# Two-layer diffusion trunk on one core: the first FFN's convolution moves to PSUM, its down-projection gets row buffers of its own, and the last FFN is ordered tile by tile

## The chip, the cores and the metric

The kernel runs on one core of a Trainium2 chip. The core has five engines that each work through their own instructions in order: TensorE (PE; its weight loads are PEld), VectorE (DVE), ScalarE (ACT), GpSimd (POOL) and SyncE (SP), which here only issues DMAs. SBUF is the core's on-chip memory of 128 partitions; PSUM is eight banks of 128 x 512 f32 into which TensorE writes its sums and which DVE and ACT read and write. The metric is device microseconds of one execution; lower is better.

## The reference

A trunk of two layers runs on 768 tokens of width 1024: 512 latent ones and 256 of context. Layer 0 mixes tokens by multi-head latent attention, layer 1 by neighbourhood attention; each mixer is followed by a gated feed-forward block (FFN) with a convolution, and each block ends with a residual sum and a layer norm:

```
def conv_ffn(h, w_in, conv_w, conv_b, w_out):
    u = h @ w_in
    u = lax.conv_general_dilated(
        u, conv_w[:, None, :].astype(u.dtype), window_strides=(1,),
        padding=[(FFN_CONV // 2, FFN_CONV // 2)],
        dimension_numbers=('NWC', 'WIO', 'NWC'),
        feature_group_count=u.shape[-1]) + conv_b
    a, g = jnp.split(u, 2, axis=-1)
    return (jax.nn.silu(g) * a) @ w_out
```

`w_in` takes 1024 to 2 x 2816 features and `w_out` 2816 back to 1024; the convolution has three taps a channel and runs over latent and context tokens apart (so 511 and 255 neighbours). The first FFN is that of layer 0, on all 768 tokens; the last is that of layer 1, on the latent 512.

## The kernel before

Everything is f32. For TensorE an operand is split in a high part (rounded by a cast on ACT) and a low part (the rest, a subtraction on DVE or POOL), and a product is three matmuls: high x high, low x high, high x low. `load` (L112) brings 1 MB of weights through SP into one of two raw buffers.

The first FFN's up-projection has the hidden width in 22 chunks. A chunk is one Strassen-Winograd step with seven products of twelve matmuls of 128x384 (`product`, L895): the feature side is split in quadrants and their sums S1 to S4 (`sums`, L834 to L837, hi/lo parts L849 and L851), the weight side in B11 to B22 and their sums T1 to T4 on DVE (`weights`, L863 to L866, casts L873 on ACT, low parts L875 on POOL). P1 and P2 add up in the PSUM tile `x`, the other five in the two halves of `yz`. ACT copies P1 from `x` to `s` (L906); DVE adds from PSUM (L903) write the chunk's two halves `ct` of 128x768.

`finish` does the convolution: ACT writes `w1*ct+b` into an SBUF tile `ut` (L927, 128x768), DVE adds the two neighbours in place (L929 and L931, each on 511 and 255 columns, for both halves: eight instructions), ACT applies Silu in place (L934), DVE multiplies the halves to `hm` (L936), and SP stores it as a row of `hid` in DRAM (L937).

The down-projection reads `hid` back: for each half of the tokens and each of eleven pairs of chunks `u`, SP loads `hr` (L971, 393 KB), ACT casts it to `hh` (L984), DVE subtracts to `hl` (L985), and 36 matmuls of 128x512 (L133 to L135, `yps`) follow. These buffers (`fd0`) lie on the left stack of SBUF, opened after the buffers of the up-projection have been closed.

The last FFN (`ffn`, L1047 to L1150) keeps its convolution's input `u` in PSUM, adds into SBUF (L1047), and ends with the sum into `acc` (L1133), the statistics (L676), and the layer norm (L1142, L1150) of four row tiles.

What stands in which order on an engine is set by the framework's scheduler, which simulates a timeline as the program is built; buffers and their number limit what it can place early.

Of the kernel before, what the change touches and what calls it, by code (L numbers as in the profile page):

```python
# [44 lines left out]
def trunk(ctx, tc, x, cx, cc, ada_w, ada_b, vec, ln1_g, ln1_b, ln2_g, ln2_b, w_in, w_out, m_in, m_qb,  # L45
# [44 lines left out]
    sil = const.tile([128, KD, 32], F32, name="sil")  # L90
    nc.vector.memset(sil, 0.0)
    nc.scalar.activation(sil[:, :, 0:2], cct, AF.Silu)
# [39 lines left out]
    def mm3(ps, ah, al, bh, bl, start, stop):  # L132
        nc.tensor.matmul(ps, ah, bh, start=start, stop=False)  # L133
        nc.tensor.matmul(ps, ah, bl, start=False, stop=False)  # L134
        nc.tensor.matmul(ps, al, bh, start=False, stop=stop)  # L135
# [84 lines left out]
    adap, close_ada = pool("adap", side="right")  # L220
    pw, close_pw = pool("pw", side="right")
# [473 lines left out]
    def to_features(z, t, s, slot, dst, wp):  # L695
# [16 lines left out]
        if not slot:  # L712
# [5 lines left out]
            else:  # L718
                sums(t % 3, nc.vector if t == 5 else nc.gpsimd)
# [49 lines left out]
    def mixer_out(layer, slot, o, w_o, nt, wl=None, us=(), done=(), banks=()):  # L769
# [10 lines left out]
        for t in range(nt):  # L780
            s = int(t >= 4)
            tl = slice(t * 128, t * 128 + 128)
            xt = wp.tile([128, D], F32, name="xr", tag="xr", bufs=2)
# [35 lines left out]
    quads, aq = {}, {}  # L819

# [9 lines left out]
    def sums(j, eng):  # L830
        j = slice(j * 128, j * 128 + 128)
        a11, a12, a21, a22 = (quads[q][:, :, j] for q in ((0, 0), (0, 1), (1, 0), (1, 1)))
        s1 = quads["S1"][:, :, j]
        eng.tensor_tensor(s1, a21, a22, op=ALU.add)  # L834
        eng.tensor_tensor(a21, a11, a21, op=ALU.subtract)
        eng.tensor_tensor(a11, s1, a11, op=ALU.subtract)
        eng.tensor_tensor(a12, a12, a11, op=ALU.subtract)  # L837

    def ffn0():
        sq, close_sq = pool("sq", side="left")  # L840
        hl = [acp.tile([128, KD * C], F32R, name="ac" + i, tag="ac" + i, bufs=1) for i in "hl"]
        aq["A22"] = [w[:, :1536].rearrange("p (k n) -> p k n", k=4) for w in hl]
        for n, (nm, q) in enumerate((("S2", (0, 0)), ("S1", "S1"), ("S3", (1, 0)), ("A22", (1, 1)), ("S4", (0, 1)))):
            if nm != "A22":
                aq[nm] = [sq.tile([128, 4, 384], F32R, name=nm + i) for i in "hl"]
            hi, lo = aq[nm]
            for j in range(3):
                sl = slice(j * 128, j * 128 + 128)
                nc.scalar.copy(hi[:, :, sl], quads[q][:, :, sl])  # L849
                e = nc.gpsimd if (n + j) % 2 else nc.vector  # L850
                e.tensor_tensor(lo[:, :, sl], quads[q][:, :, sl], f(hi[:, :, sl]), op=ALU.subtract)  # L851
# [4 lines left out]
        def weights(c, nm):  # L856
            if c not in raws:
                raws[c] = load(w_in[0, c])
            q = {n: raws[c][:, 512 * i:512 * i + 512] for i, n in enumerate(("B11", "B12", "B21", "B22"))}
            if nm[0] == "T" and c not in tts:  # L860
                tt = hp.tile([128, 3, 512], F32, name="tt", tag="tt", bufs=2)
                t3, t2, t4 = (tt[:, i] for i in range(3))
                nc.vector.tensor_tensor(t3, q["B22"], q["B12"], op=ALU.subtract)  # L863
                nc.vector.tensor_tensor(t2, t3, q["B11"], op=ALU.add)
                nc.vector.tensor_tensor(q["B12"], q["B12"], q["B11"], op=ALU.subtract)
                nc.vector.tensor_tensor(t4, q["B21"], t2, op=ALU.subtract)  # L866
                tts[c] = {"T1": q["B12"], "T2": t2, "T3": t3, "T4": t4}
# [6 lines left out]
            e = nc.vector if c < 2 and nm in ("B21", "T1", "T4") else nc.gpsimd  # L874
# [3 lines left out]
        def product(c, p):  # L878
            a, b = PRODUCTS[p]
            wh, wl = weights(c, b)  # L880
            ah, al = aq[a]
# [10 lines left out]
            for k in range(4):  # L892
                ks = slice(k * 128, k * 128 + 128)
                for m, (w, x_) in enumerate(((wh, ah), (wl, ah), (wh, al))):
                    nc.tensor.matmul(ps, w[:, ks], x_[:, k], start=first and k == 0 and m == 0,  # L895
                                     stop=k == 3 and m == 2, skip_group_check=True)

            def tmp(nm):
                d[nm] = hp.tile([128, 384], F32, name=nm, tag=nm, bufs=2)
# [20 lines left out]
        def finish(c):  # L920
            cw = vt[:, CW + c * 6:CW + c * 6 + 6]
            cb = vt[:, CB + c * 2:CB + c * 2 + 2]
            ut = [None, None]
            for i in (1, 0):
                p = prod[c]["c", i]
# [609 lines left out]
```

## Time and profile before

| what | value |
|---|---|
| median of 3 runs | 1858.76 us (1855.51 to 1859.38) |
| profiled execution, its own time | 1858.97 us |
| its span | 1857.0 us |
| busy PE / DVE / POOL / ACT in the span | 91% / 66% / 54% / 48% |
| mixer's output of layer 0 ends, first FFN's products begin | 493.74 us |
| first FFN, last up product | 897.61 us |
| first FFN, first down product | 917.16 us |
| span's last DVE instructions | from 1851.39 us |

A row of a timeline gives the start, the duration, engine, line, operation, and output and inputs by the program's names; x2 is two such instructions in a row; in brackets stands the idle time of the engine before it and the one that released it. A row of a line's group gives the duration of one as least, median and most in ns.

### The profile page before, as it was taken

The page shows a single profiled execution, that of the slowest core. Times are in us where ns is not written, and L with a number is a line of the kernel's source. Part 1 is how long each engine was busy: PE and PEld are TensorE (multiplying, and loading weights), DVE is VectorE, ACT ScalarE, POOL GpSimd, SP SyncE. Part 2 cuts the span into 40 slices and gives each one's busy share as a digit, 9 for nine tenths or more (in the row PEclk, how much of TensorE's full clock was granted, in tenths as well). Part 3 has the DMA queues.
Part 4 walks back from the last instruction along what each step waited for, and adds up shares of the span by engine and source line. Part 5 has one row for each costly group of instructions (what it writes and reads, how often), then busy time and mean ns, then how long its engine had stood idle before and what let it go on. Part 6 is the DMA issues. An engine that isn't in the chain of part 4 may idle for free. (4 is left out here: it accounts for less than half of the span.)

```text
span 1857.0 us, 25938 instructions
## 1 busy us (share of the span) xinstructions
PE 1697.8 (91%) x9512; PEld 1472.1 (79%) x9512; DVE 1220.5 (66%) x2086; ACT 891.1 (48%) x1800; POOL 1010.9 (54%) x913
## 2 busy tenths in 40 slices
PE   6999999989778988998499998899998899999996
PEld 4887787878678988888388778899887788888875
DVE  4477777785688888888615443667664834465776
ACT  3366666672544444434234435676673444333431
POOL 3224334242665656656465946687694745467442
PEclk8999999999989999999799998999998899999998
DMA  8224455234212221222555442111113423223321
GB/s 312 101 103 171 157 196 194 108 115 153 75 46 94 94 91 67 92 94 94 200 171 188 170 145 89 54 55 55 52 55 103 173 88 109 96 79 138 112 80 46
DMA packets 46583, 214.21 MB, mean 115 GB/s; under 512 B 4952, under 2 KB 13032, under 8 KB 28408
## 3 DMA queue, kind: packets, MB, share of 16 engines
q1 hardware_dynamic: 43288, 202.07, 30.8%
q10 hardware_dynamic: 3168, 10.49, 1.6%
q8 instruction: 75, 1.23, 0.3%
q14 instruction: 52, 0.43, 0.1%
HBM read 194.42 MB, written 18.15 MB: 114 GB/s over the span
## 5 line engine op out<-in xcount | busy, mean ns | idle before, releaser
L129 POOL TENSOR_TENSOR wl<-raw,wh 128x512 fp32r<-128x512 f32 x246 | 332.0, 1380 | 195.8 <-ACT wh L125 195.6
L125 ACT CAST wh<-raw 128x512 fp32r<-128x512 f32 x272 | 149.3, 621 | 118.3 <-PE u L134 68.8
L875 POOL TENSOR_TENSOR wl<-raw,wh 128x512 fp32r<-128x512 f32 x84 | 126.9, 1524 | 82.5 <-ACT wh L873 82.5
L493 POOL TENSOR_SCALAR e<-e,st 128x768 f32<-128x768 f32 (+1 forms) x96 | 75.4, 786 | 168.1 <-DVE st L492 143.4
L133 PE MATMUL u<-axh,wh 128*128 128x512 f32 (+1 forms) x384 | 143.8, 375 | 4.4 <-DVE z L800 3.3
L134 PE MATMUL u<-axl,wh 128*128 128x512 f32 (+1 forms) x384 | 143.6, 375 | 0.6 <-POOL axl L732 0.6
L135 PE MATMUL u<-axh,wl 128*128 128x512 f32 (+1 forms) x384 | 143.4, 374 | 0.0
L875 POOL TENSOR_TENSOR wl<-tt,wh 128x512 fp32r<-128x512 f32 x64 | 93.4, 1472 | 58.8 <-ACT wh L873 58.8
L133 PE MATMUL yps<-wh,hh 128*128 128x512 f32 x264 | 106.5, 403 | 19.2 <-ACT hh L984 19.2
L134 PE MATMUL yps<-wl,hh 128*128 128x512 f32 x264 | 105.5, 400 | 0.0
L985 DVE TENSOR_TENSOR hl<-hr,hh 128x128 fp32r<-128x128 f32 (+2 forms) x55 | 38.1, 744 | 101.6 <-ACT hh L984 101.6
L135 PE MATMUL yps<-wh,hl 128*128 128x512 f32 x264 | 104.3, 397 | 0.0
L929 DVE SCALAR_TENSOR_TENSOR ut<-ct,vt,ut 128x511 f32<-128x511 f32 x88 | 87.2, 1031 | 16.1 <-ACT ut L927 16.0
L511 DVE TENSOR_TENSOR pl<-ptr,ph 128x512 fp32r<-128x512 f32 x112 | 76.3, 687 | 21.8 <-ACT ph L507 20.3
L931 DVE SCALAR_TENSOR_TENSOR ut<-ct,vt,ut 128x511 f32<-128x511 f32 x88 | 89.5, 1047 | 0.0
L133 PEld LDWEIGHTS u<-axh,wh 128*128 128x128 f32 x384 | 73.3, 191 | 17.3 <-DVE z L800 3.5
L134 PEld LDWEIGHTS u<-axl,wh 128*128 128x128 f32 x384 | 73.4, 191 | 13.5 <-POOL axl L732 0.9
L487 ACT ACTIVATE e<-sc,st 128x768 f32<-128x768 f32 (+1 forms) x96 | 73.7, 767 | 21.6 <-PE ptr L500 10.2
L135 PEld LDWEIGHTS u<-axh,wl 128*128 128x128 f32 x384 | 73.3, 191 | 12.5
L480 DVE TENSOR_REDUCE st<-sc 128x1 f32<-128x768 f32 (+1 forms) x96 | 73.8, 774 | 14.3 <-PE sc L135 13.4
L507 ACT CAST ph<-ptr 128x512 fp32r<-128x512 f32 x112 | 64.4, 587 | 36.7 <-PE ptr L500 28.2
L1133 DVE TENSOR_TENSOR acc<-ops,acc 128x512 f32<-128x512 f32 x72 | 48.4, 684 | 49.6 <-PE ops L135 49.4
(576 smaller groups left out, 5638.5 us busy)
## 6 DMA issues: line engine op xcount, KB each, us to landing
raw<-w_in SPq DMA_DIRECT2D x44, 1024.0 KB
raw<-ada_w SPq DMA_DIRECT2D x40, 1024.0 KB
raw<-w_out SPq DMA_DIRECT2D x33, 1024.0 KB
raw<-n_qkv SPq DMA_DIRECT2D x12, 1024.0 KB
hid<-hm SPq DMA_DIRECT2D x22, 384.0 KB
hr<-hid SPq DMA_DIRECT2D x22, 384.0 KB
rr<-resid ACTq DMA_DIRECT2D x10, 512.0 KB
raw<-ada SPq DMA_DIRECT2D x4, 1024.0 KB
```

The costliest lines, as they stand in the source:

```text
L125: nc.scalar.copy(hi[:, a:b], raw[:, a:b])
L129: e.tensor_tensor(lo[:, a:b], raw[:, a:b], f(hi[:, a:b]), op=ALU.subtract)
L133: nc.tensor.matmul(ps, ah, bh, start=start, stop=False)
L134: nc.tensor.matmul(ps, ah, bl, start=False, stop=False)
L135: nc.tensor.matmul(ps, al, bh, start=False, stop=stop)
L480: nc.vector.tensor_reduce(st[:, 0:1], ps[:, :n], axis=AX.X, op=ALU.max, negate=True)
L487: done["a"] = nc.scalar.activation(e[:, :n], ps[:, :n], AF.Exp, bias=st[:, 0:1], scale=1.0, accum_out=st[:, 1:2]).ins
L493: done["p"] = nc.gpsimd.tensor_scalar(e[:, :n], e[:, :n], st[:, 2:3], 1.0, op0=ALU.mult, op1=ALU.mult).ins
L511: nc.vector.tensor_tensor(pl, tr, f(ph), op=ALU.subtract)
L875: e.tensor_tensor(lo, src, f(hi), op=ALU.subtract)
L929: nc.vector.scalar_tensor_tensor(u[:, a + 1:b], p[:, a:b - 1], cw[:, 3 * i:3 * i + 1], u[:, a + 1:b], op0=ALU.mult, op1=ALU.add)
L931: nc.vector.scalar_tensor_tensor(u[:, a:b - 1], p[:, a + 1:b], cw[:, 3 * i + 2:3 * i + 3], u[:, a:b - 1], op0=ALU.mult, op1=ALU.add)
```

## The change

- `finish`: the convolution's running value lies in PSUM: `ul` (two banks, 512 latent columns of each half) and `uc` (one bank, 256 context columns of both). ACT's two instructions of 768 columns become four of 512 and 256, Silu reads PSUM and writes `hm` in two pieces, and DVE multiplies `hm` by the other half in PSUM in two pieces. `uc` shares its two banks with `x`.
- `fd`, the down-projection's row buffers, is opened first, below those of the up-projection, with one `hr` in place of two and two `hh`/`hl` in place of three.
- `sums` gives S1, S3, S2, S4 in this order (S2 is now a22 - S3), the last tile's sums stand in `ffn0` between the splits, S1, S2 and S4 are split on DVE, S3 and A22 on POOL, and P5 comes before P6 in the first two chunks.
- `tp`, a pool opened before the mixer's last part, holds `tt` and `s1`, and T4 is written over B21 just before P4; `w_in` is laid out B11, B12, B22, B21.
- In layer 0 `xr` has one buffer in place of two, and `sil` lies in another pool.
- In the last FFN the products of a later row tile are issued after the last one of the tile before.

The diff, cut to its core (the new lines are some 14 to 20 higher: L895 is now L910, L929 and L931 are L946 and L948, L984 is L1001):

```diff
@@ sums @@
-        eng.tensor_tensor(s1, a21, a22, op=ALU.add)
-        eng.tensor_tensor(a21, a11, a21, op=ALU.subtract)
-        eng.tensor_tensor(a11, s1, a11, op=ALU.subtract)
-        eng.tensor_tensor(a12, a12, a11, op=ALU.subtract)
+        for nm, dst, x_, y_, op in (("S1", quads["S1"][:, :, j], a21, a22, ALU.add),
+                                    ("S3", a21, a11, a21, ALU.subtract), ("S2", a11, a22, a21, ALU.subtract),
+                                    ("S4", a12, a12, a11, ALU.subtract)):
+            eng.tensor_tensor(dst, x_, y_, op=op)
+            yield nm
@@ ffn0 @@
+        fd, close_fd = pool("fd0", side="left")
         sq, close_sq = pool("sq", side="left")
...
+        for nm in sums(2, nc.vector):
+            if nm == "S1":
+                split("S1", nc.vector, 3)
+            elif nm == "S2":
+                split("S2", nc.vector, 3)
+                split("S3", nc.gpsimd, 3)
+        split("A22", nc.gpsimd, 3)
+        split("S4", nc.vector, 3)
@@ weights @@
-                tt = hp.tile([128, 3, 512], F32, name="tt", tag="tt", bufs=2)
+                tt = tp.tile([128, 2, 512], F32, name="tt", tag="tt", bufs=2)
...
+            if nm == "T4":
+                nc.vector.tensor_tensor(q["B21"], q["B21"], tts[c]["T2"], op=ALU.subtract)
@@ finish @@
-                ut[i] = u = hp.tile([128, T], F32, name=f"ut{i}", tag=f"ut{i}", bufs=2)
-                nc.scalar.activation(u, p, AF.Identity, bias=cb[:, i:i + 1], scale=cw[:, 3 * i + 1:3 * i + 2])
...
-                if i:
-                    nc.scalar.activation(u, u, AF.Silu)
+            ul = [bank("ul", [128, 512], "tr") for i in range(2)]
+            uc = bank("uc", [128, 512])
+            ut = [[(ct[i][:, :S], ul[i]), (ct[i][:, S:], uc[:, C * i:C * i + C])] for i in range(2)]
             for i in (1, 0):
+                for p, u in ut[i]:
+                    n = u.shape[-1]
+                    nc.scalar.activation(u, p, AF.Identity, bias=cb[:, i:i + 1], scale=cw[:, 3 * i + 1:3 * i + 2])
+                    nc.vector.scalar_tensor_tensor(u[:, 1:], p[:, :n - 1], cw[:, 3 * i:3 * i + 1], u[:, 1:],
+                                                   op0=ALU.mult, op1=ALU.add)
+                    nc.vector.scalar_tensor_tensor(u[:, :n - 1], p[:, 1:], cw[:, 3 * i + 2:3 * i + 3], u[:, :n - 1],
+                                                   op0=ALU.mult, op1=ALU.add)
-            nc.vector.tensor_tensor(hm, ut[0], ut[1], op=ALU.mult)
+            for a, b, k in ((0, S, 0), (S, T, 1)):
+                nc.scalar.activation(hm[:, a:b], ut[1][k][1], AF.Silu)
+                nc.vector.tensor_tensor(hm[:, a:b], hm[:, a:b], ut[0][k][1], op=ALU.mult)
@@ down-projection @@
-                hm = hp.tile([128, 2, 384], F32, name="hr", tag="hr", bufs=2)
+                hm = fd.tile([128, 2, 384], F32, name="hr", tag="hr", bufs=1)
...
-                hh, hl = (hp.tile([128, 2, 384], F32R, name="h" + i, tag="h" + i, bufs=3) for i in "hl")
+                hh, hl = (fd.tile([128, 2, 384], F32R, name="h" + i, tag="h" + i, bufs=2) for i in "hl")
@@ ffn, the products of the last layer's down-projection @@
-                    mm3(pls[t_][hf], hh[:, tt], hl[:, tt], wh[:, b:b + 512], wl[:, b:b + 512], c == c0, c == c1 - 1)
+                    with ExitStack() as es_:
+                        if final and behind and c == c0 and t_ > 1:
+                            es_.enter_context(tc.issue_after(behind[0]))
+                        behind[:] = [mm3(pls[t_][hf], hh[:, tt], hl[:, tt], wh[:, b:b + 512], wl[:, b:b + 512],
+                                         c == c0, c == c1 - 1)]
```

The first place is DVE in the middle of the up-projection, where `finish` of one chunk meets the sums of the next chunk's weights. The names are those of the text above; a number behind a name tells one buffer's use from another. Before:

```order
L931 SCALAR_TENSOR_TENSOR ut_7313<-ct_7100,vt,ut_7313 128x511
L936 TENSOR_TENSOR hm<-ut_7174,ut_7167 128x768
L931 SCALAR_TENSOR_TENSOR ut_7313<-ct_7100,vt,ut_7313 128x255
L903 TENSOR_TENSOR ct_7101<-yz,s_7135 128x384
L863 TENSOR_TENSOR tt<-raw 128x512
L903 TENSOR_TENSOR s_7367<-yz,s_7251 128x384
L864 TENSOR_TENSOR tt<-tt,raw 128x512
L929 SCALAR_TENSOR_TENSOR ut_7306<-ct_7101,vt,ut_7306 128x511
```

And after:

```order
L946 SCALAR_TENSOR_TENSOR ul<-ct_7293,vt,ul 128x511
L946 SCALAR_TENSOR_TENSOR ul<-ct_7292,vt,ul 128x511
L948 SCALAR_TENSOR_TENSOR ul<-ct_7293,vt,ul 128x511
L946 SCALAR_TENSOR_TENSOR uc<-ct_7437,vt,uc 128x255
L948 SCALAR_TENSOR_TENSOR ul<-ct_7292,vt,ul 128x511
L948 SCALAR_TENSOR_TENSOR uc<-ct_7437,vt,uc 128x255
L918 TENSOR_TENSOR s_7614<-yz,s_7594 128x384
L953 TENSOR_TENSOR hm<-hm,ul 128x512
L918 TENSOR_TENSOR ct_7436<-yz,s_7450 128x384
L877 TENSOR_TENSOR tt<-raw 128x512
L878 TENSOR_TENSOR raw<-raw 128x512
L879 TENSOR_TENSOR tt<-tt,raw 128x512
```

The eight additions are as many as before; what moved is their third operand, from SBUF (`ut`) to PSUM (`ul`, `uc`), and the sums of the weights now stand together.

The second place is ACT at the first FFN's start (f: the features' quadrants and their sums; S1h and the like: high parts; `s`: the copy of P1). Before:

```order
L710 ACTIVATE f_5225<-ltr,comb 128x128 x4
L849 CAST S2h<-f_5222 128x4x128 x2
L849 CAST S1h<-fs 128x4x128 x2
...
L849 CAST S4h<-f_5223 128x4x128
L906 COPY s_5776<-x 128x384
L906 COPY s_5813<-x 128x384
L873 CAST wh<-tt 128x512 x3
```

And after:

```order
L888 CAST wh<-raw 128x512 x6
L888 CAST wh<-tt 128x512 x4
...
L921 COPY s_5782<-x 128x384
L855 CAST ach<-f_5228 128x4x128
L921 COPY s_5819<-x 128x384
L888 CAST wh<-raw 128x512 x3
L710 ACTIVATE f_5227<-ltr,comb 128x128 x4
L710 ACTIVATE f_5228<-ltr,comb 128x128 x4
L888 CAST wh<-tt 128x512
L855 CAST S1h<-fs 128x4x128 x2
```

The copies of P1 and the casts of the first two chunks' weight sums moved ahead of the splits.

The third place is ACT at the first casts of the down-projection's rows. Before, they are behind the last Silu of the up-projection:

```order
L934 ACTIVATE ut_8786<-ut_8786 128x768
L984 CAST hh<-hr 128x2x256
L984 CAST hh<-hr 128x2x8x8 x2
L984 CAST hh<-hr 128x2x256
```

And after, they stand in the third chunk's `finish`:

```order
L921 COPY s_6158<-x 128x384
L888 CAST wh<-raw 128x512 x4
L1001 CAST hh<-hr 128x2x256
L1001 CAST hh<-hr 128x2x8x8 x2
L945 ACTIVATE uc<-ct_6054,vt 128x256
```

The casts of `u` = 0 moved by some nineteen chunks; those of `u` = 1 follow two chunks later.

## Rows read from the trace of the kernel before

**Rows 1.** Windows: us and busy us (instructions) PE, PEld, DVE, ACT, POOL; clock; DMA.
```profile
609.18:878.25 269.07, 243.17 (x1349) 233.16 (x1348) 231.36 (x287) 117.68 (x192) 161.84 (x111) 1.00 0.24 87
1467.00:1800.00 333.00, 325.92 (x1514) 271.59 (x1513) 196.02 (x236) 131.49 (x231) 191.28 (x137) 0.99 0.32 116
```

**Rows 2.** Timeline of SP's queue: first and last of 17 stores, then the row loads.
```profile
609.18 0.33 SPq L937 DMA_DIRECT2D hid<-hm  x1
...
878.25 0.33 SPq L937 DMA_DIRECT2D hid<-hm  x1
...
911.20 18.81 SPq L971 DMA_DIRECT2D hr<-hid  x6
```

**Rows 3.** Timeline of PE, at the first FFN's waits.
```profile
493.74 0.33 PE L895 MATMUL x<-axh,wh 128*128 128x384 f32 x1
...
494.26 0.35 PE L895 MATMUL x<-axh,wh 128*128 128x384 f32 x1
...
520.16 0.69 PE L895 MATMUL x<-axh,wh 128*128 128x384 f32 x1 [15.88 <-ACT s L906]
...
526.40 0.34 PE L895 MATMUL x<-axh,wl 128*128 128x384 f32 x1
...
897.61 0.34 PE L895 MATMUL yz<-S4l,wh 128*128 128x384 f32 x1
917.16 0.80 PE L133 MATMUL yps<-wh,hh 128*128 128x512 f32 x1 [19.22 <-ACT hh L984]
...
922.40 0.40 PE L133 MATMUL yps<-wh,hh 128*128 128x512 f32 x1
922.63 0.40 PE L134 MATMUL yps<-wl,hh 128*128 128x512 f32 x1
```

**Rows 4.** Timeline of DVE in the up-projection.
```profile
642.38 3.21 DVE L931 SCALAR_TENSOR_TENSOR ut<-ct,vt,ut 128x511 f32<-128x511 f32 x2
645.51 1.14 DVE L929 SCALAR_TENSOR_TENSOR ut<-ct,vt,ut 128x511 f32<-128x511 f32 x2
...
649.53 0.54 DVE L903 TENSOR_TENSOR ct<-yz,s 128x384 f32<-128x384 f32 x1
...
655.40 1.77 DVE L865 TENSOR_TENSOR raw<-raw 128x512 f32<-128x512 f32 x1
```

**Rows 5.** Timeline of POOL beside them.
```profile
640.44 4.87 POOL L875 TENSOR_TENSOR wl<-raw,wh 128x512 fp32r<-128x512 f32 x3
647.49 3.25 POOL L875 TENSOR_TENSOR wl<-tt,wh 128x512 fp32r<-128x512 f32 x2 [2.18 <-ACT wh L873]
```

**Rows 6.** Groups by line in 493:898: busy us, mean ns, idle before.
```profile
L929 DVE SCALAR_TENSOR_TENSOR ut<-ct,vt,ut 128x511 f32<-128x511 f32 x86 | 86.0, 1041 | 15.0 <-ACT ut L927 14.9
L865 DVE TENSOR_TENSOR raw<-raw 128x512 f32<-128x512 f32 x22 | 21.6, 980 | 0.0
```

**Rows 7.** Lines alone: ns least/median/most, first and last start, forms.
```profile
L903 DVE TENSOR_TENSOR ct<-yz,s x66: 542/549/559, 542.2 to 898.8; 128x384 f32<-128x384 f32 x66
L1047 DVE SCALAR_TENSOR_TENSOR ut<-u,vt,ut x44: 733/749/752, 1497.0 to 1824.0; 128x511 f32<-128x511 f32 x44
L1045 ACT ACTIVATE ut<-u,vt x44: 770/777/782, 1496.2 to 1823.1; 128x512 f32<-128x512 f32 x44
```

**Rows 8.** Timeline of DVE at the first FFN's start.
```profile
506.40 0.69 DVE L834 TENSOR_TENSOR fs<-f,f 128x512 f32<-128x512 f32 x1 [4.14 <-ACT f L710]
...
518.86 0.68 DVE L851 TENSOR_TENSOR S4l<-f,S4h 128x512 fp32r<-128x512 f32 x1
```

**Rows 9.** Timeline of DVE at the end of the program.
```profile
1843.74 1.23 DVE L1133 TENSOR_TENSOR acc<-ops,acc 128x512 f32<-128x512 f32 x2
...
1847.68 1.27 DVE L676 BATCH_NORM_STATS2 bn<-acc 128x6 f32<-128x512 f32 x2
...
1851.39 2.40 DVE L1150 SCALAR_TENSOR_TENSOR acc<-acc,rs,bc_eb 128x512 f32<-128x512 f32 x2
```

**Rows 10.** Timeline of PE at its last matmul.
```profile
1842.50 0.40 PE L135 MATMUL ops<-wzh,hl 128*128 128x512 f32 x1
```

More of the change, by code (lines that the diff above doesn't have):

```diff
@@ L134, in mm3 @@
         nc.tensor.matmul(ps, ah, bl, start=False, stop=False)
-        nc.tensor.matmul(ps, al, bh, start=False, stop=stop)
+        return nc.tensor.matmul(ps, al, bh, start=False, stop=stop).ins
     def wide(src, xw, eng):
@@ L220, in trunk @@
     adap, close_ada = pool("adap", side="right")
+    sil = adap.tile([128, KD, 32], F32, name="sil")
+    nc.vector.memset(sil, 0.0)
+    nc.scalar.activation(sil[:, :, 0:2], cct, AF.Silu)
     pw, close_pw = pool("pw", side="right")
@@ L717, in to_features @@
                     nc.gpsimd.tensor_tensor(lo, quads[0, i][:, :, j], f(hi), op=ALU.subtract)
-            else:
-                sums(t % 3, nc.vector if t == 5 else nc.gpsimd)
+            elif t < 5:
+                for _ in sums(t % 3, nc.gpsimd):
+                    pass
             return
@@ L839, in ffn0, with split @@
     def ffn0():
+        fd, close_fd = pool("fd0", side="left")
         sq, close_sq = pool("sq", side="left")
[L841 to L844, printed above, removed]
+        def split(nm, eng, pieces):
+            if nm == "A22":
+                hl = [acp.tile([128, KD * C], F32R, name="ac" + i, tag="ac" + i, bufs=1) for i in "hl"]
+                aq[nm] = [w[:, :1536].rearrange("p (k n) -> p k n", k=4) for w in hl]
+            else:
@@ L845, in ffn0 @@
                 aq[nm] = [sq.tile([128, 4, 384], F32R, name=nm + i) for i in "hl"]
             hi, lo = aq[nm]
[L847 to L851, printed above, removed]
+            n = 384 // pieces
+            for j in range(pieces):
+                sl = slice(j * n, j * n + n)
+                nc.scalar.copy(hi[:, :, sl], quads[SRC[nm]][:, :, sl])
+                eng.tensor_tensor(lo[:, :, sl], quads[SRC[nm]][:, :, sl], f(hi[:, :, sl]), op=ALU.subtract)
@@ L893, in product @@
                 ks = slice(k * 128, k * 128 + 128)
+                ah, al = (w[:, k] for w in aq[a])
                 for m, (w, x_) in enumerate(((wh, ah), (wl, ah), (wh, al))):
-                    nc.tensor.matmul(ps, w[:, ks], x_[:, k], start=first and k == 0 and m == 0,
+                    nc.tensor.matmul(ps, w[:, ks], x_, start=first and k == 0 and m == 0,
                                      stop=k == 3 and m == 2, skip_group_check=True)
             def tmp(nm):
-                d[nm] = hp.tile([128, 384], F32, name=nm, tag=nm, bufs=2)
+                d[nm] = (tp if nm == "s1" else hp).tile([128, 384], F32, name=nm, tag=nm, bufs=2)
                 return d[nm]
@@ L954, in ffn0 @@
         e1 = affine(wp, ln1_g[0:1], ln1_b[0:1])
-        hp, close_hp = pool("fd0", side="left")
         a2 = new_a(1)
@@ L1103, in down @@
                          for c in cs] + order[4 * (c1 - c0):]
-            pls, left = {}, {}
+            pls, behind = {}, []
             if last:
```

35 lines of the change are left out of this document (13 added, 22 removed).

## The prediction

> **What bounds the kernel now.** I read the busy table first, then the windows by stage, the timelines of PE's waits, and those of DVE and POOL in the stretch with most of them. TensorE is busy 91% of the span, so the question is where the other 9% lie and what it waits for there. In the first FFN's up-projection four matmuls in a row start 0.52 us apart, first to last, 0.173 each at full clock [rows 3]; its 22 x 84 = 1848 would fill 319.7 us. They take 404.2, from 493.74 to 897.95 [rows 3]: 84.5 us are waits and half-speed matmuls. The same view of the last FFN shows a fed PE, 325.9 busy of 333 [rows 1].
>
> They lie in three places. At the start PE stands 15.88 us, until 520.16, named for ACT's copy `s`; the 19 matmuls from there to 526.40 take 6.24 us, on the lower of the two clocks, where 19 x 0.173 = 3.3 would do: 2.9 more [rows 3]. In the middle 17 stores of `hid`, 609.18 to 878.25, give 269.07/16 = 16.82 us for a chunk, where 84 x 0.173 = 14.53 would do: 2.29 us lost a chunk, 13.6% [rows 2]. After the last product PE waits 19.22 us for `hh`, since SP issues the `hr` loads at 911.20 only, and the first 12 matmuls take 5.24 us where 12 x 0.23 = 2.76 would do, 2.5 more at half clock [rows 2, 3].
>
> Who holds the middle back is DVE, 231.4 of 269.1 us busy, 86% [rows 1]: it adds the products from PSUM and frees the banks. And it is that busy because it shares something with POOL. The pair of additions at 642.38 takes 3.21 us while POOL runs three subtractions back to back, 640.44 to 645.31; the next pair, at 645.51 with POOL idle, takes 1.14. At 649.53 POOL works again, and DVE's add with one operand in PSUM takes 0.54 [rows 4, 5]. That add lies between 542 and 559 ns all 66 times, whatever POOL does; the additions with all operands in SBUF average 1041 over their two lengths, and the last FFN's, with PSUM on one side, are 733 to 752 for the longer one alone [rows 6, 7].
>
> **The change part by part.** *Convolution in PSUM.* Eight additions a chunk at 1.04 us are 8.3 us [rows 6]. Now one input lies in PSUM, as with L903 and L1047 [rows 7], so four pairs should cost 4 x 1.14 = 4.6 [rows 4]: 3.7 us less. Two multiplications for one add some 0.1. The four sums of weights keep both inputs in SBUF; each lies between 0.68 (the last of rows 8, of the same size) and 1.77 [rows 4], 2.7 to 7.1 us a chunk, and is now up to 0.98 at the mean [rows 6], at most 3.9 in all. DVE has 231.36/16 = 14.46 us a chunk [rows 1]; it keeps 14.46 - 3.7 + 0.1 = 10.9, and I add 0.5 for sums of weights that meet POOL more often: 11.4, or 78% of 14.53. ACT gets three instructions more a chunk; at no more than the 0.78 of a whole 512 columns [rows 7] that is 2.3 us on an engine that is 44% busy there [rows 1], and hidden.
>
> [...]
>
> How much of PE's 2.29 us a chunk goes? Two windows bound it: DVE at 86% with 13.6% lost, and at 59% (196.0/333) with PE idle 2.1% [rows 1, 2]. A straight line between them gives 8% lost with DVE at 72%. Bounds: 0 (all waits go) and 13.6% (none). I take 4%, nearer to the fed window, because the products now come in one regular row (P1, P6, P4 of the chunk before, P2, P5, P3 of the chunk before, P7, nearly always twelve matmuls each), which leaves an add two products, 24 x 0.173 = 4.2 us, before its result is needed.
>
> *Start.* P1 and P2 of the first two chunks need only what is ready before the last tile's sums; before, P2 waited for `s`. So 48 matmuls are done by about 503, and 1800 are left behind the wait where before 1824 were. The next, P5, needs the third part of S1l, the tenth DVE instruction from 506.40 on, when the last features come. The twelve that stood there before took 518.86 + 0.68 - 506.40 = 13.1 us, 1.09 each [rows 8]; ten take 10.9: P5 at 517.3 (with ten at 0.68 or 1.77: 513 to 524). The 2.9 us of half clock behind the wait stay. The stage ends at 517.3 + 2.9 + 1800 x 0.173/0.96 = 844.6; with nothing lost 831.6, with 13.6% 880.6. Against 897.95 that is **-53.5** (-66 to -17).
>
> *Row buffers of their own.* The loads and casts of `u` = 0 and 1 now stand in the up-projection, so the down-projection can follow the last product: its sums in `yz`'s banks wait for nothing, those in the banks of `x` and `uc` for the last `uc`, some 5 us that other sums fill. Of 19.2 + 2.5 us I leave 2.2 for that: **-19.5** (-22 to -12). The price: some 4 us of DVE work in the up-projection, in its slack, and three `hr` loads in SP's row behind a store each; a raw load behind them may come 2 us late, three times. With one `hr` and two `hh`, the load, cast and subtraction of the next rows must fit in 36 x 0.23 = 8.3 us. They have time for that, but on POOL six halves of the residual's sums now stand among the weights' low parts at the start. I put **+2** on it all (0 to +8).
>
> *Last FFN.* DVE has a backlog at the end: the last matmul is issued at 1842.50, yet norms and statistics of earlier tiles stand before the last tile's, whose statistics start at 1847.68 and whose last step ends at 1853.79 [rows 9, 10]. Tile by tile, two tiles are done 48 matmuls (11 us) before the end and the third 24 (5.5 us). What then stands behind 1842.9 is the add of 1.23, statistics of 1.27, small steps of 0.4 and two norm steps, of 2.40 each at most [rows 9]: 1850.6. **-3.2** (-5 to 0).
>
> *The rest.* One `xr` in place of two: the load is issued behind the use before, a few us ahead of its own; nothing, at most 2. T4 in place holds the raw buffer until P4's cast, no longer than P3's B22 did. `sil` and `tp` only move memory.
>
> Sum: -53.5 - 19.5 + 2 - 3.2 = -74. It is made against the profiled execution's own 1858.97 (span 1857.0 and 2.0 around it), 0.2 over the median of the runs, so nothing is to be corrected: **1785 us**. Its own range, with 0 to 8% lost (8%: 858.7, 14 later) and the transition's bounds, is 1768 to 1803.
>
> **The rivals.** *DVE stays the bound.* What was lost to POOL on the additions is lost on the sums of weights, which now stand in a row: at 1.77 each, 7.1 against 3.9, they give back 3.2 of the 3.7 us. For it: L865 in rows 4; against it: POOL is busy only 60% of the stretch (161.84/269.07, rows 1). The chunk then keeps about 16.8 us and the stage only what the earlier start and the ends give, the 17 of the bound: 1859 - 17 - 19.5 + 2 - 3.2 = 1821. *It doesn't do what it says:* the additions stay slow, since no row shows them with their output in PSUM and POOL's subtractions of this stage beside them, and the waits at the stage's ends stay too, so that only the earlier start counts (520.16 to 517.3): 1859 - 2.9 - 19.5 + 2 - 3.2 = 1835. *Slower: one set of PSUM tiles.* `ul` has two banks for both halves, so ACT can't begin a chunk's convolution before DVE has multiplied the one before, and each hands to the other again and again. With no overlap at all the loop is 3.1 (ACT's four at 0.78 at most) + 4.6 + 1.2 (Silu) + 1.1 (products) + five adds of 0.55 + 7.1 for sums of weights at 1.77 = 19.8 us a chunk, 520.2 + 21.43 x 19.8 = 944.5, 46.6 later than now, less 20.7 for the other parts: 1885. It decides from 18.6 us a chunk on, where 520.2 + 21.43 x 18.6 is 20.8 over 897.95. Against it: only the additions of one column part hang on each other, and adds and sums of weights stand between.
>
> **How the numbers follow.** The forecast 0.63; DVE stays the bound 0.15; the additions stay slow 0.08; one set of tiles, slower, 0.08; 0.06 for mixtures that land near 1859. A difference under 0.2% (3.7 us) can't be told from no change. The first three are faster, 0.86, with one hundredth of the mixtures 0.87; 0.04 of them lie within 0.2%; the slower one and the last hundredth make 0.09. The range, 1766 to 1836, runs from the forecast's low end over the two rivals on the fast side and leaves out the slower one and most mixtures.
>
> **What would show it.** Right: additions of 511 and 255 columns in the up-projection with a spread as narrow as L903's; stores of `hid` 15.0 to 15.5 us apart; P5 at about 517; under 3 us before the first down product and no half clock behind it; DVE's last instruction some 8 us after the last matmul. Wrong: PE waits named for ACT's `ul` or `uc`, sums of weights near 1.77 us each, a wait on `hh` in the third or fourth `u`, or stores over 16 us apart.

## The result: 1806.5 us, 2.7% faster, and the profile after

The changed kernel takes 1806.51 us (median of 4 runs, 1805.22 to 1808.49), the one before 1857.91 beside it: a ratio of 0.9726, 95% interval 0.9709 to 0.9742. The forecast was 1785 with a range of 1766 to 1836: right in its direction and inside the stated range, and 21 us too low. The measured time lies over the range that the forecast gives itself (1768 to 1803), and inside the stated one because that reaches up to the two rivals on the fast side, 1821 and 1835; so what speaks for the forecast is not the number but the stages below. The gain is 51 us where 74 were forecast; the two profiled spans, by which the parts are counted below, differ by 50.4.

The convolution did what the sum said. First the windows, of the whole middle of the up-projection, from one store of `hid` to the seventeenth after it (us; busy us of PE, PEld, DVE, ACT and POOL; clock; DMA share; GB/s), to be held against [rows 1, 2]:

```profile
602.19:856.59 254.40, 247.74 (x1413) 244.72 (x1413) 201.13 (x322) 134.74 (x254) 154.29 (x114) 1.00 0.30 100
```

254.40/17 is 14.96 us a chunk, against 16.82 before and 14.53 for a PE that never waits. DVE is down from 14.46 to 11.83 us a chunk (11.4 was forecast), 79% busy. Then the lines of the additions alone (ns least, median and most), which answer to [rows 6, 7]:

```profile
L946 DVE SCALAR_TENSOR_TENSOR uc<-ct,vt,uc x44: 472/483/489, 543.8 to 858.1; 128x255 f32<-128x255 f32 x44
L946 DVE SCALAR_TENSOR_TENSOR ul<-ct,vt,ul x44: 739/748/757, 553.2 to 865.5; 128x511 f32<-128x511 f32 x44
...
L948 DVE SCALAR_TENSOR_TENSOR ul<-ct,vt,ul x44: 742/749/756, 554.6 to 866.8; 128x511 f32<-128x511 f32 x44
```

No addition is over 757 ns, though POOL is busy 61% of that stretch. The sums of weights, which keep two inputs in SBUF, still meet it; their groups in 528:856 have means of 900, 959, 1262 and 1267 ns, up to nearly twice the uncontended 0.68 us:

```profile
L882 DVE TENSOR_TENSOR raw<-raw,tt 128x512 f32<-128x512 f32 x20 | 25.3, 1267 | 4.2 <-POOL wl L890 4.1
L879 DVE TENSOR_TENSOR tt<-tt,raw 128x512 f32<-128x512 f32 x19 | 24.0, 1262 | 0.0
```

What PE still waits for behind the start, 534 to 864 us, is named for DVE's adds `ct` (nine waits, 9.3 us in all), none of it for `ul` or `uc`.

What went wrong stands in PE's timeline. At the start (start, duration, in brackets the idle time before and who ended it), first the last tile's transposes before, beside [rows 3]:

```profile
502.40 1.88 PE L707 MATMUL ltr<-ident,z 128*128 128x128 f32 x8 [3.44 <-DVE z L686]
```

And after:

```profile
510.70 1.97 PE L707 MATMUL ltr<-ident,z 128*128 128x128 f32 x8 [7.50 <-DVE z L686]
520.52 0.69 PE L910 MATMUL yz<-S1h,wh 128*128 128x384 f32 x1 [7.86 <-ACT S1h L855]
...
528.35 0.69 PE L910 MATMUL yz<-S1l,wh 128*128 128x384 f32 x1 [6.17 <-DVE S1l L856]
```

The last tile's transposes come at 510.70, where before they came at 502.40, and P5 runs through from 528.35 on, not from 517.3. DVE's timeline there, against [rows 8], shows the weights' work ahead of the last tile's sum (L801) and norm (L686), one of them waiting for its load. Two of them are low parts of T2, which the change also moves from POOL to DVE in the first two chunks (T1's go the other way; the list of the change leaves this out):

```profile
494.44 3.47 DVE L890 TENSOR_TENSOR wl<-tt,wh 128x512 fp32r<-128x512 f32 x2
497.84 1.78 DVE L890 TENSOR_TENSOR wl<-raw,wh 128x512 fp32r<-128x512 f32 x1
499.54 1.28 DVE L801 TENSOR_TENSOR z<-yps,bc_g 128x512 f32<-128x512 f32 x2
...
507.45 1.52 DVE L877 TENSOR_TENSOR tt<-raw 128x512 f32<-128x512 f32 x1 [2.71 <-DMA raw<-w_in]
508.90 1.75 DVE L686 TENSOR_SCALAR z<-z,mv,rs 128x1024 f32<-128x1024 f32 x1
...
515.59 0.68 DVE L838 TENSOR_TENSOR fs<-f,f 128x512 f32<-128x512 f32 x1
...
527.62 0.68 DVE L856 TENSOR_TENSOR S1l<-fs,S1h 128x512 fp32r<-128x512 f32 x1
```

And PE in the down-projection and behind it:

```profile
850.72 0.39 PE L130 MATMUL yps<-wh,hh 128*128 128x512 f32 x1
...
883.80 0.51 PE L132 MATMUL yps<-wh,hl 128*128 128x512 f32 x1 [2.17 <-DVE hl L1002]
...
1067.06 1.94 PE L707 MATMUL ltr<-ident,a 128*128 128x128 f32 x8 [5.64 <-DVE a L686]
1071.70 0.58 PE L130 MATMUL vps<-wh,axh 128*128 128x256 f32 x1 [2.71 <-ACT axh L731]
```

The first down product now runs 12.6 us before the last up product ends, at a granted clock of 1.00 (36 of them stand among the last up products), so the wait of 19.22 us is gone, and with it the 5.24 us at 0.51 behind it. But four waits for `hl` of over 1 us have come, 9.3 us in all with a short one, and the next layer's first product comes 16.7 us after the last down product (1054.99), where before it was 10.3 (1109.71 to 1119.97). In the first half of the tokens this stands on DVE in front of the product that waits at 883.80, though the cast of its row had ended at 879.08 (L981 multiplies the residual's rows):

```profile
876.62 5.45 DVE L981 TENSOR_TENSOR rr<-rr,bc_eg 128x1024 f32<-128x1024 f32 x3 [3.58 <-POOL bc_eg L766]
882.00 4.34 DVE L1002 TENSOR_TENSOR hl<-hr,hh 128x512 fp32r<-128x512 f32 x3
```

And in the second half, in front of the wait of 2.15 us that ends at 967.02, where the cast had ended at 960.91:

```profile
961.55 2.31 DVE L981 TENSOR_TENSOR rr<-rr,bc_eg 128x1024 f32<-128x1024 f32 x1
963.79 0.20 DVE L678 BATCH_NORM_AGGREGATE mv<-bn 128x2 f32<-128x12 f32 x1
963.91 3.06 DVE L1002 TENSOR_TENSOR hl<-hr,hh 128x384 fp32r<-128x384 f32 x2
```

A table of the milestones, in us of each profiled span (after, the last up product ends behind the 36 down products, some 8.3 us, that stand among the last up products):

| | before | after | gained up to there |
|---|---|---|---|
| first up product | 493.74 | 493.84 | -0.1 |
| last up product ends | 897.95 | 863.32 | 34.6 |
| last down product ends | 1109.71 | 1054.99 | 54.7 |
| next layer's first product | 1119.97 | 1071.70 | 48.3 |
| last matmul ends | 1842.89 | 1795.26 | 47.6 |
| span ends | 1857.01 | 1806.66 | 50.4 |

### The profile page after: what moved, and what is told of

The parts are those of the page before. It is cut to its first block, busy times and chain, and to the rows that moved or that the text cites. A ratio compares the mean times of both kernels' runs of the same rounds, so it can differ in the third digit from the quotient of the medians.

```text
span 1806.7 us, 26070 instructions
## 1 busy us (share of the span) xinstructions
PE 1685.0 (93%) x9512; PEld 1466.1 (81%) x9512; DVE 1185.1 (66%) x2109; ACT 904.7 (50%) x1866; POOL 995.0 (55%) x912
## 5 line engine op out<-in xcount | busy, mean ns | idle before, releaser
L126 POOL TENSOR_TENSOR wl<-raw,wh 128x512 fp32r<-128x512 f32 x246 | 335.4, 1394 | 190.1 <-ACT wh L122 189.7
L122 ACT CAST wh<-raw 128x512 fp32r<-128x512 f32 x272 | 149.2, 620 | 118.4 <-PE u L131 69.0
L890 POOL TENSOR_TENSOR wl<-raw,wh 128x512 fp32r<-128x512 f32 x106 | 148.0, 1417 | 71.0 <-ACT wh L888 71.0
L1002 DVE TENSOR_TENSOR hl<-hr,hh 128x128 fp32r<-128x128 f32 (+2 forms) x55 | 55.3, 1049 | 82.8 <-ACT hh L1001 82.8
L890 POOL TENSOR_TENSOR wl<-tt,wh 128x512 fp32r<-128x512 f32 x42 | 58.4, 1392 | 54.0 <-ACT wh L888 33.1
L888 ACT CAST wh<-raw 128x512 fp32r<-128x512 f32 x110 | 62.5, 618 | 50.7 <-PE yz L910 30.7
L487 ACT ACTIVATE e<-sc,st 128x768 f32<-128x768 f32 (+1 forms) x96 | 73.6, 767 | 21.3 <-PE ptr L500 10.1
L132 PEld LDWEIGHTS u<-axh,wl 128*128 128x128 f32 x384 | 73.5, 192 | 12.6
L1154 DVE TENSOR_TENSOR acc<-ops,acc 128x512 f32<-128x512 f32 x72 | 48.4, 686 | 47.5 <-PE ops L132 47.2
L1064 DVE SCALAR_TENSOR_TENSOR ut<-u,vt,ut 128x511 f32<-128x511 f32 x44 | 32.8, 746 | 66.6 <-ACT ut L1062 66.6
```

The costliest lines, as they stand in the source:

```text
L122: nc.scalar.copy(hi[:, a:b], raw[:, a:b])
L126: e.tensor_tensor(lo[:, a:b], raw[:, a:b], f(hi[:, a:b]), op=ALU.subtract)
L132: return nc.tensor.matmul(ps, al, bh, start=False, stop=stop).ins
L487: done["a"] = nc.scalar.activation(e[:, :n], ps[:, :n], AF.Exp, bias=st[:, 0:1], scale=1.0, accum_out=st[:, 1:2]).ins
L888: nc.scalar.copy(hi, src)
L890: e.tensor_tensor(lo, src, f(hi), op=ALU.subtract)
```

## The experiments

Theory: with every operand in SBUF the additions block and are blocked by POOL; PSUM takes them out of that. Rival: the products' regular order brought the gain. Then, for the 23 us that are missing: what holds the start, what makes the waits for `hl`, and what the 6.4 us behind the down-projection. All runs but the last have four times, the last five; each is set against runs of the kernel before on its own chip (medians 1857.9 to 1859.6). The first up product comes between 491.3 and 493.9 us in all these traces, also where the edit lies far behind it (e5 and e7, edits of the down-projection: 491.7 and 491.3, against 493.8 in the changed kernel); so differences of under 3 us between the times of two traces decide nothing here.

**e1, the changed kernel with the running value in SBUF again.**

```diff
-            ul = [bank("ul", [128, 512], "tr") for i in range(2)]
-            uc = bank("uc", [128, 512])
+            ul = [hp.tile([128, 512], F32, name="ul", tag=f"ul{i}", bufs=1) for i in range(2)]
+            uc = hp.tile([128, 512], F32, name="uc", tag="uc", bufs=2)
```

> The changed kernel with one thing undone: the convolution's running value (ul, uc) lies in SBUF tiles, in the same pieces of 512 and 256 columns and with the same instructions on the same engines. Theory (with all operands in SBUF an addition blocks and is blocked by POOL's subtractions): the additions of 511 columns spread from 0.75 to about 1.9 us again, their mean over both lengths is back near 1.0, DVE is back over 85% busy in the middle of the up-projection, stores of hid stand 16.2 to 16.8 us apart in place of 14.96, and the time is 22 to 38 us over the changed kernel's 1806.5: 1829 to 1845. Rival (the regular order of the products and sums brought the gain, not the place of the value): stores stay within 0.3 us of 14.96 and the time within 6 us of 1806.5.

Measured: 1845.0 us, ratio 0.9929 (0.9915 to 0.9944): 38.5 over the changed kernel, at the upper end of the theory's range. The same line of additions as above, now:

```profile
L946 DVE SCALAR_TENSOR_TENSOR uc<-ct,vt,uc x44: 471/482/1519, 545.3 to 894.1; 128x255 f32<-128x255 f32 x44
L946 DVE SCALAR_TENSOR_TENSOR ul<-ct,vt,ul x44: 736/749/1894, 549.9 to 900.7; 128x511 f32<-128x511 f32 x44
```

The least and the median are those of PSUM to a few ns, the most is 1.9 us: SBUF does not make an addition slower, meeting POOL does. In the kernel before, where the value lies in SBUF too, 79 of the 176 additions take over 0.8 us (511 columns) or 0.55 us (255), and all 79 have work of POOL beside them over at least 58% of their time; the 84 that have none end within 752 ns. In the changed kernel 100 of the 176 have it beside them over nine tenths of their time, and none is slow. The chunk is 17.55 us (fifteen from 601.43 to 864.69), longer even than before and than the 16.8 that was expected at most, and DVE is 91% busy from 609.18 to 878.25:

```profile
609.18:878.25 269.07, 243.00 (x1328) 236.33 (x1327) 244.83 (x306) 130.91 (x239) 167.24 (x110) 0.97 0.25 90
```

The last up product ends 35.8 us later than in the changed kernel, the last down product 38.2: that is the price of the place, for the additions and for the two multiplications (L953) that read the running value, and the rival is out.

**e2, the kernel before with that part alone.** The edit is the `finish` of the change, in the old kernel.

> The kernel before with one part of the change alone: the convolution's running value in PSUM, in pieces of 512 and 256. Theory: the additions are free of POOL's work (739 to 757 and 472 to 489 ns), the stores of hid come 15.0 to 15.3 us apart in place of 16.82, and the time falls by 28 to 40 us, to 1818 to 1830; the 15.9 us at the start and the 19.2 us before the down-projection stay. Rival (the order of products was needed for it): less than 12 us gained.

Measured: 1829.0 us, ratio 0.9840 (0.9825 to 0.9854): 30.6 us gained. The additions are 739 to 756 and 474 to 491 ns, the chunk 15.5 us. The part alone carries 31 of the 51 us, without the other order. The sums of weights rose to means of 0.76 to 1.41 us here, which may be why the chunk came out 0.2 to 0.5 us over what was expected; that was not tested.

**e3, the row buffers opened late again.** Two `hr` and three `hh` and `hl`, behind the up-projection.

```diff
-        fd, close_fd = pool("fd0", side="left")
         sq, close_sq = pool("sq", side="left")
...
         e1 = affine(wp, ln1_g[0:1], ln1_b[0:1])
+        fd, close_fd = pool("fd0", side="left")
```

> The changed kernel with the down-projection's row buffers opened after the up-projection again, with two hr and three hh and hl as before. Theory: the wait of about 19 us for the first hh and some 2.5 us of half clock return, and the waits for hl in the down-projection (2.2, 1.2, 3.5 and 2.2 us, with some 2 us of half clock behind them) go, since they come from the shorter row of buffers: 9 to 14 us slower than the changed kernel, 1815 to 1821. Rival (those waits come from the residual's sums on DVE and POOL, not from the buffers): they stay, and it is 18 to 22 us slower, 1824 to 1829.

Measured: 1813.3 us, ratio 0.9758 (0.9742 to 0.9774), 6.8 over the changed kernel. The first wait is back, and behind it there is no wait for `hl` in either half:

```profile
875.37 0.79 PE L130 MATMUL yps<-wh,hh 128*128 128x512 f32 x1 [20.53 <-ACT hh L1001]
```

With the deeper buffers the rows are cast and subtracted ahead, and the residual's sums (L981) do no harm, in the second half at least; in the first they lie within the 20.5 us. In the first half a pair's three subtractions, which take 2.8 to 4.3 us in the changed kernel where POOL works beside them, take 1.10 here:

```profile
894.40 1.10 DVE L1002 TENSOR_TENSOR hl<-hr,hh 128x512 fp32r<-128x512 f32 x3 [7.30 <-ACT hh L1001]
```

In the second half they meet POOL here too (2.10 and 3.23 us for two at 969.82 and 979.97, 1.03 alone), and yet no product waits: there it is the number of buffers that ends the waits.

The gain of the early buffers is 6.8 us and not the 17.5 of the sum. It was less than expected even of undoing it, as the distance to the next layer is 10.3 us here again: the early buffers, or their number, brought the 6.4 us of e5 along.

**e4 and e6, the start: holding weight work behind the last tile's norm.** e4 holds it on DVE:

```diff
+            hold = ExitStack()
+            if c >= 2 or nm in ("T2", "T4"):
+                hold.enter_context(tc.issue_after(z5))
```

> The changed kernel with the weight work that is not needed before the products P5 (T2 and T4 of the first two chunks, everything of later chunks) held on DVE behind the last row tile's norm. Theory (the first FFN starts late because DVE does that work ahead of the last tile's residual sum and norm): the last features come near 504 to 506 in place of 514.8, P5 runs through from 519 to 523 in place of 528.35, and the time falls by 5 to 9 us: 1797 to 1801. Rival (POOL's subtractions and the lock between the two engines set the start whatever the order): P5 moves by less than 3 us and the time stays within 3 us of 1806.5.

e6 holds the work of everything but B11 and B21 on both engines, on POOL behind the last norm's power:

```diff
+            if c >= 2 or nm not in ("B11", "B21"):
+                hold.enter_context(tc.issue_after(z5))
+                hold.enter_context(tc.issue_after(rs5))
```

> As e4, and in addition on POOL the same weight work held behind the power that the last tile's norm needs. In e4 DVE reached the norm early, but POOL gave that power 4.6 us after DVE asked for it. Theory (POOL's row of work, ahead of that one small instruction, is what holds the start): the power comes within 1.5 us of DVE's request, the features of the last tile before 507, P5 runs through from 518 to 522, the last up product ends 6 to 10 us before the changed kernel's 863.3. Rival (the lock between DVE and POOL sets the pace of the splits whatever comes first): P5 not before 524.5 and the stage's end within 6 us of 863.3.

Measured: e4 1805.4 us (ratio 0.9715, 0.9701 to 0.9730), e6 1808.1 (0.9730, 0.9716 to 0.9745). In e4 the last transposes ran 4.9 us earlier and P5 2.6 us:

```profile
525.75 0.69 PE L916 MATMUL yz<-S1l,wh 128*128 128x384 f32 x1 [6.23 <-DVE S1l L857]
```

The last up product ended 5.1 us earlier. But the next layer's mixer, unchanged in its code, came out in another order: from its last head to the last FFN it took 50.5 us in place of 42.6, 7.9 more, and the last FFN made up only 5.0 of them. In e6 the transposes ran at 501.43, 9.3 us earlier, and yet:

```profile
528.22 0.69 PE L917 MATMUL yz<-S1l,wh 128*128 128x384 f32 x1 [7.43 <-DVE S1l L857]
```

An early norm alone is not enough, and both theories fall. The numbers of both rivals came in, but e6 also moved T1's sums behind the norm, so its rival is not shown by it, and e9 speaks against e4's ("whatever the order"). DVE's timeline of e6 shows what stood in front: between the norm (498.54) and the last part of S1l are 22 sums and subtractions, 13 of them at some 1.75 us. What both rivals call a lock shows in the trace as these times alone: 1.75 us with POOL at work beside them, 0.68 from 523.88 on, while POOL stands idle from 523.40 to 532.54:

```profile
517.16 1.76 DVE L857 TENSOR_TENSOR S1l<-fs,S1h 128x512 fp32r<-128x512 f32 x1
518.85 1.75 DVE L857 TENSOR_TENSOR S2l<-f,S2h 128x512 fp32r<-128x512 f32 x1
...
526.28 1.28 DVE L896 TENSOR_TENSOR wl<-raw,wh 128x512 fp32r<-128x512 f32 x2
527.49 0.68 DVE L857 TENSOR_TENSOR S1l<-fs,S1h 128x512 fp32r<-128x512 f32 x1
```

**e9, S1's parts in front.**

```diff
+                s1 = split("S1", nc.vector, 3)
+                behind_s1.enter_context(tc.issue_after(s1))
...
+            if c >= 2 or nm not in ("B11", "B21", "T1"):
+                hold.enter_context(tc.issue_after(s1))
+                hold.enter_context(tc.issue_after(rs5))
```

> The changed kernel with S1's parts first at the start: on DVE the other sums and splits of the last row tile and the weight work that P5 does not need stand behind the last part of S1l, on POOL that weight work stands behind the last norm's power. In e4 and e6 the norm came 6 to 10 us earlier, yet the last part of S1l ended at 525.7 and 528.2, as it stood behind some fifteen subtractions of 1.75 us. Theory (its place in DVE's row is what holds P5): P5 runs through from 509 to 514 in place of 528.35; P6 then waits for S2l and T2's low part, so of the 15 us some 6 to 10 are left at the last up product, which ends at 853 to 858 (863.32), and the time is 1796 to 1801. Rival (all of that work must be done before the products can run on, in whatever order): the waits move from P5 to P6 and P7, and the last up product ends within 3 us of 863.3.

Measured: 1799.0 us, ratio 0.9680 (0.9666 to 0.9694), 7.6 under the changed kernel. P5 and P6 of e9:

```profile
511.11 0.69 PE L920 MATMUL yz<-S1l,wh 128*128 128x384 f32 x1 [0.75 <-DVE S1l L857]
...
522.16 0.69 PE L920 MATMUL yz<-S2h,wh 128*128 128x384 f32 x1 [5.38 <-ACT S2h L856]
```

P5 runs from 511.1, 17 us earlier, P6 waits 5.4 us for S2, and the last up product ends at 855.9, 7.4 us earlier (2.2 us of both are there at the first up product already). What stands in DVE's row ahead of the last part of S1l held the start, in front of the norm as in the changed kernel or behind it as in e6; more than half of the gain moves on to P6 and what follows, as both theory and rival had in part. e9 has the early norm of e6 as well. S1 in front with the late norm was not run: from the first sum at 515.59 and the 6.6 us between that sum and P5 in e9 (504.55 to 511.11), an estimate gives P5 at 522, 6 us earlier.

**e5, the end of the down-projection tile by tile.**

```diff
+                                    if u == FC // 2 - 1 and n and prev:
+                                        es_.enter_context(tc.issue_after(prev[n - 1]))
```

> The changed kernel with the last two pairs of chunks of each half of the first down-projection multiplied row tile by row tile. In the changed kernel the first product of the next layer comes 16.7 us after the last down product, before it was 10.3. Theory (in the changed kernel the three tiles' sums end within 7 us of each other, so DVE reaches the last tile's residual sum and norm late): the distance falls back to 10 to 11 us and the time by 5 to 7 us, to 1799.5 to 1801.5. Rival (the distance comes from buffers or loads, not from the order): it stays over 15 us and the time within 2 us of 1806.5.

Measured: 1797.9 us, ratio 0.9670 (0.9646 to 0.9694), its four runs 1790.0 to 1800.9. The transposes before the next layer:

```profile
1050.09 1.94 PE L707 MATMUL ltr<-ident,a 128*128 128x128 f32 x8 [2.64 <-DVE a L686]
1054.95 0.58 PE L130 MATMUL vps<-wh,axh 128*128 128x256 f32 x1 [2.93 <-ACT axh L731]
```

The distance is 10.2 us again, where the changed kernel has 16.7. The theory holds for these 6.5 us; the waits for `hl` also fell, from 9.3 to 5.7 us, which was not expected; the profiled run is the fastest of the four. In the changed kernel the last tile's sum stands 4.3 us behind the last product, and its last wait is for the store of an earlier tile, which frees one of the two buffers `a`:

```profile
1059.32 1.29 DVE L1020 TENSOR_TENSOR a<-yps,bc_g 128x512 f32<-128x512 f32 x2 [0.95 <-DMA resid<-a]
1060.52 2.35 DVE L1021 TENSOR_TENSOR a<-rr,a 128x512 f32<-128x512 f32 x2
```

In e5 that sum starts at 1044.27, 0.4 us before the last product ends (1044.71), and the pair of additions behind it takes 1.28.

**e7, row loads cut in two, three half buffers.**

```diff
-                hm = fd.tile([128, 2, 384], F32, name="hr", tag="hr", bufs=1)
+                hms = [fd.tile([128, 384], F32, name="hr", tag="hr", bufs=3) for _ in range(2)]
```

> The changed kernel with the row loads of the down-projection cut in two, one chunk each, in three buffers of half the size, which fit beside the rest. Theory (with one hr buffer the load, cast and subtraction of a pair must follow each other, 3.3 + 1.0 + 4.0 us and the ways between them, over the 8.3 us of its products): the four waits for hl, 9.0 us in all, fall under 3 us, and the time by 6 to 10 us, to 1796.5 to 1800.5. Rival (the subtractions are slow because POOL blocks them, whatever the buffers): more than half of the waits stay and the time falls by less than 4 us.

Measured: 1802.5 us, ratio 0.9702 (0.9686 to 0.9719), 4 under the changed kernel. Two of the waits for `hl` stayed, 2.5 and 1.9 us in the second half, and the first two broke into several of under 0.8 us: 6.4 us in all where 9.3 were, so the expected gain is missed. By its numbers the rival came in, with the time at its limit of 4 us; that POOL alone makes the waits does not follow, as e3 has none. With `hl` double, an extra half of `hr` is not enough; while POOL adds the residual's sums and subtracts, DVE takes 18.11 us for 18 subtractions of half the size, three pairs of chunks (6.0 us a pair):

```profile
880.14 18.11 DVE L1002 TENSOR_TENSOR hl<-hr,hh 128x256 fp32r<-128x256 f32 x18
```

**e8 and e10, edits together.** e8 is e5, e6 and e7; e10 is e5 and e9.

> The changed kernel with the edits of e5, e6 and e7 together. If the three places are apart from each other the gains add up: 16 to 24 us under the changed kernel, 1782 to 1791. If one of them only moves the wait to the next place (the start's gain is eaten by a later order of the mixer, or the rows' loads get in the weights' way), under 12 us: over 1794.

> e9 and e5 together. If both hold and are apart: e5's 8.6 us and e9's 5 to 10 add up, 1787 to 1793. If e9 gives nothing: 1796 to 1801.

Measured: e8 1801.0 us (0.9691, 0.9677 to 0.9706), e10 1802.1 (0.9693, 0.9677 to 0.9709): neither faster than e5 alone (the three intervals overlap). e8 misses the sum of its parts, and where it lost them stays open. In e10 the gains did add up to the next layer, whose first product came 14.4 us before the changed kernel's; then that layer's mixer lost 4.6 us between its last head and the last FFN, and some 4 more in the parts on either side.

**e12, as e10, the tile order in the second half alone.**

```diff
-                                    if u == FC // 2 - 1 and n and prev:
+                                    if u == FC // 2 - 1 and n and prev and not th:
```

> As e10, but with the tile order only in the second half of the tokens, at whose end the next layer waits. In e10 the two gains did not add up: up to the next layer they did (its first product 14.4 us earlier than in the changed kernel), then the next layer's mixer, whose code is the same, came out in another order and lost 4.6 us between its last head and the last FFN, and 2 us more in either neighbour. Theory (that loss is the scheduler's other order, not the edits): with that part in the order of e5 and e9 the distance is 42 to 43 us again and the time 1788 to 1795, below both e5 and e9. Rival (an earlier start collides with something else later on): over 1797.

Measured: 1793.4 us (five runs, 1791.7 to 1794.5), ratio 0.9651 (0.9638 to 0.9664), the lowest median of all (only e5's interval overlaps): 13 us under the changed kernel. The mixer's last part has the same 150 matmuls in the same order as the changed kernel and e5, and takes 42.6 us as there (47.2 in e10, in another order); P5 comes at 511.9, the next layer's first product 10.3 us behind the last down product. So e10's loss there goes with the scheduler's order.

**e11, the last FFN in the scheduler's own order.** The condition on the last products is set to never.

> The changed kernel with the last FFN's products in the scheduler's own order again, as before the change. Theory (DVE had a backlog at the end since the four row tiles' sums ended close together): the span ends 13.5 to 14.5 us after the last matmul in place of 11.4, 2 to 3.5 us slower than the changed kernel, 1808.5 to 1810. Rival (the gain at the end came from another part): no difference, within 1 us in the span's end behind the last matmul.

Measured: 1809.0 us, ratio 0.9729 (0.9712 to 0.9745). The span ends 14.1 us behind the last matmul, as before, in place of 11.4: the theory's 2.7 us, inside one run's scatter in the total.

## Why the prediction was right, and where it was 21 us off

- **Convolution in PSUM: right, mechanism and size.** 4 x 1.14 us were forecast for four pairs and 748 + 483 ns less the overlap are what came (1.14 us for the two from 642.54 to 643.68); 4% lost in PE was taken and 2.9% measured in the middle (14.96 against 14.53). e1 and e2 show from both sides that the place of the running value does it. With one input in SBUF an addition of 511 columns takes 757 ns at most here, whatever POOL does; with two (e1) it reaches 1894. That the running value lies in PSUM costs no time that shows: 739 to 757 ns there and 736 ns at least with it in SBUF (e1).
- **Start: the step that failed.** "The next, P5, needs the third part of S1l, the tenth DVE instruction from 506.40 on": the first sum of the features did not start at 506.40 but at 515.59, 9.2 us later, as the weights' work of the first chunks stood in front of the last tile's sum and norm; and from there the last S1l was not 10.9 but 12.7 us off, since six of the ten took some 1.75 us. The sum counted the instructions behind the features and not those moved ahead of them. It cost 11.0 us of the 53.5. The half clock behind the wait was forecast to stay, and did: 0.50 from 520.16 to 526.40 before, 0.57 from 528.35 to 534.60 after. e9 shows that it is DVE's row ahead of S1l that held P5; an early norm with that work behind it (e6) gains nothing.
- **Row buffers: right in kind, too large by 5 us.** No wait and no half clock before the first down products, as forecast, but 9.3 us of waits for `hl` where 4.2 were allowed. "They have time for that" left nothing over: a load of 3.3 us, a cast of 1.0 and contended subtractions of 4.0 took 8.0 us (886.37 to 894.34) of the 8.3, and where DVE did nothing else, 895 to 941, no product waited. The waits came where the residual's products (L981) and norms stood on DVE between cast and subtraction. e3 shows that deeper buffers end them, with the residual's work still there in the second half; the residual's place alone was not tested.
- **Not in the sum: 6.4 us before the next layer.** The new order of the down-projection ended the three row tiles' sums within 7 us, and the last tile's norm came late. The sum left out that an order can change at the end of the step; e5 shows it. e3, with the buffers late and more of them, has the 10.3 us too.
- **Last FFN: right.** 3.2 us were forecast, 2.7 came, and e11 gives back 2.7.
- 11.0 at the start + 5.2 for the rows + 6.4 before the next layer + 0.5 at the end + 0.7 elsewhere are 23.8; 23.6 lie between the 74 forecast and the 50.4 of the two spans. The forecast's own range, worked out again from 0 to 8% lost and -22 to -12 for the rows, is 1769 to 1807 and not 1768 to 1803; the measured time lies at its upper end.
- **The rivals.** DVE did not stay the bound: the sums of weights rose to means of 0.90 to 1.27 us, not to 1.77, beside a POOL that works 9.1 us a chunk where it worked 10.1. The additions did not stay slow (757 ns at most). One set of PSUM tiles was no bottleneck; the chunk is 14.96 us, far from 18.6.

## What to carry to other kernels

Where DVE and POOL both work from SBUF, look at the spread of one line, not at its mean: a median of 0.75 with a maximum of 1.9 us is a collision here, and moving the running operand to PSUM ended it. When a step is moved ahead, count what now stands in front of the old work on that engine, and look at both ends of the moved region. And where a scheduler orders the program, compare edits stage by stage: e4 was 6.2 us ahead at the next layer's first product and then lost 7.9 in a part that it didn't touch, of which 5.0 came back.

## What the runs showed of the hardware that was not expected

With the running value in SBUF and split in two pieces (e1) the chunk took 17.5 us, longer than the 16.82 before, though its additions average 0.91 us over both lengths where they averaged 1.04 before. What grew on DVE are the two multiplications, 1.9 us a chunk where one of 768 columns took 1.0 before and two with an input in PSUM take 1.1 in the changed kernel, and the sums of weights, 4.6 us a chunk where they took 3.2; why they meet POOL so often there stays open. And POOL feels the collision too: its subtractions have a median of 1298 ns in e2, where only the convolution was changed, and 1478 in the kernel before (each kernel's line alone, the same 84 instructions of 128x512). Over the windows of the middle above, all of POOL's instructions take 1.52 us each in e1 (167.24/110), 1.46 in the kernel before (161.84/111) and 1.35 in the changed kernel (154.29/114). The lines of e2 and of the kernel before:

```profile
L875 POOL TENSOR_TENSOR wl<-raw,wh x84: 1277/1298/1844, 486.0 to 843.7; 128x512 fp32r<-128x512 f32 x84
```

```profile
L875 POOL TENSOR_TENSOR wl<-raw,wh x84: 1283/1478/1766, 486.5 to 872.5; 128x512 fp32r<-128x512 f32 x84
```
